# Sums of squares of the memory tokens moved from GpSimd to VectorE and to later attention steps, and one half projection moved between the first two steps

## The chip, the cores and the metric

One Trainium2 chip, one core of it. The metric is device time in microseconds (us) of one execution of the whole program, the median of a few runs. The engines that matter are TensorE (PE in the profile; its weight loads are PEld), VectorE (DVE), ScalarE (ACT), GpSimd (POOL) and the queue from which transfers are issued (SP). Each engine takes its own instructions in the order in which they stand in its queue, and an instruction that waits for another engine holds up all that stand behind it.

## The reference, cut to what matters

```python
h = rms_norm(x, norm_mix)                       # x: 512 tokens of 1024
q_a, k_a, v_a, u_b, gate_b, gate_c, g_a, g_b = split(h @ w_in)
o_a = stick_breaking_attention(q_a, k_a, v_a)   # 8 heads of 64, causal
y_b = gate_b * conv3(gate_c * u_b)
merged = sigmoid(g_a) * (o_a @ w_branch_a) + sigmoid(g_b) * (y_b @ w_branch_b)
x = x + merged @ w_mix_out
x = x + memory_cross_attention(rms_norm(x, norm_mem_q), rms_norm(mem, norm_mem_kv), ...)
x = x + swiglu(rms_norm(x, norm_ffn));  return rms_norm(x, norm_final)

# stick-breaking weights, z = q.k / 8, s < t:
# A[t,s] = exp(log_sigmoid(z_ts) + sum over s<j<t of log_sigmoid(-z_tj))

# rms_norm(mem): mem is 256 tokens of 1024, so for each token the mean of its
# 1024 squares is needed
```

Everything is float32. The change concerns two things in it: where and when the squares of `mem` are summed, and when the projections `h @ w_in` are made that lie between the steps of the attention.

## The kernel before, in words

A float32 operand of a matmul is split into a rounded part "hi" and the rest "lo" (two instructions, a cast on ScalarE and a subtraction on VectorE: L150 and L151 for weights, L169 and L170 for activations, L369 and L370 inside the attention), and a product is made of three matmuls, hi·hi, hi·lo and lo·hi (`mm3`, L155 to L157).

**The attention** runs over `steps` (L341): 4 pairs of heads, and for each pair the four key blocks `kt` = 3, 2, 1, 0, so 16 steps, numbered 0 to 15. Key block `kt` is met by queries from `kt`·128 on: 128, 256, 384 or 512 queries for each head. Up to 256 queries both heads of a pair share one PSUM bank `z`; above that each head has its own. For one step the work is this:

- `scores` (L373): matmuls into `z` (L382 or L389); then on ScalarE Abs, Exp and Ln (L396 to L398), on VectorE the softplus `e` (L399), on GpSimd the causal mask on `e` (`affine_select`, L355); ScalarE copies row 0 of `z` to a small carry (L406).
- `parts` (L408): VectorE adds the carry of the key block before (L420), then `e` is split into `l` hi (ScalarE, L369) and `l` lo (VectorE, L370).
- `weights` (L428): for each bank two matmuls with a triangle of -1, first with `l` hi, then with `l` lo (L433); VectorE forms the carry (L438) which a small DMA moves (L444); ScalarE takes Exp (L441), GpSimd masks (L355), VectorE splits the result `a` into `ah` and `al` (L449, L450).
- `values` (L454): the matmuls with v (L461).

In the main loop (L519) step `i` issues, in this order: a share of projections (`fill_some`, L524), `scores` of step i+1, `weights` of step i, `parts` of step i+1, `values` of step i-1. So the chain from the scores of a step to its `l` lo lies beside the projections that stand between them in TensorE's queue. The queue of TensorE is in the order written (`manual_schedule`, L518); those of the other engines are ordered by the Tile scheduler.

**The projections** are a list `fill` of 44 entries (L492 to L505): for each projection one entry that loads its weights and makes the first four of eight k-blocks (`open_project`, 12 matmuls, L270) and one that makes the other four (12 matmuls) and evicts on VectorE. The order is q and k of the next pair (`qk_part`, evicted by L294), then for the convolution gate C, u and gate B (`conv`: L315; L321, L322, L324, L328; L334, L335). `FILL` (L33) says how many entries stand in front of each step: (3, 2, 3, 3) for the first pair, (2, 2, 3, 4) for the other three. The 44 shares add up to the 44 entries, so a share is a number of entries. q and k of the second pair take entries 0 to 3, gate C entries 4 and 5. Before, step 0 has the whole of q and the first half of k; step 1 the second half of k and the first half of gate C.

**The memory squares** (`mem_square`, L480): at the steps in `MEM_AT` (L30: 1, 3, 5, 7) a quarter of `mem` (128x512: two blocks of 128x256) is loaded through SP (L477), squared on ScalarE in place (L484) and added to `accm` (128x256) on GpSimd, block by block (a copy, L487, and seven adds, L489). At step 12 (`MEAN_AT - 2`, L523) `squares_mean` splits `accm` (L180, L181) and the mean is made of it at step 14.

Of the kernel before, what the change touches and what calls it, by code (L numbers as in the profile page):

```python
# [8 lines left out]
F32 = mybir.dt.float32  # L9
F32R = mybir.dt.float32r  # L10
AF = mybir.ActivationFunctionType
ALU = mybir.AluOpType

P = 128
D = 1024
S = 512
KD = D // P
# [4 lines left out]
MEM = 256  # L22
MT = MEM // P
# [3 lines left out]
HS = S // 2  # L27
EPS = 1e-6
HOLD = 4
MEM_AT = (1, 3, 5, 7)  # L30
MEAN_AT = 14
EARLY = 2
FILL = ((3, 2, 3, 3), (2, 2, 3, 4))  # L33
WARM = 8
FIRST = 4

# [4 lines left out]
def hybrid_layer(ctx: ExitStack, tc: tile.TileContext, xT_d, memT_d, cols_d, wv_d, win_d,  # L41
                 wbr_d, wmix_d, wmq_d, wmk_d, wmv_d, wmo_d, wfi_d, wfo_d, out):
    nc = tc.nc
# [10 lines left out]
    lpool = stick.enter_context(tc.tile_pool(name="lpool", bufs=4))  # L54
# [8 lines left out]
    def unit(s, cols=512):  # L63
        return upool.tile([P, cols], F32R, tag="u", name=nm(s), padded_shape=[P, 512])
# [4 lines left out]
    def f(ap):  # L69
        return ap.bitcast(F32)  # L70
# [42 lines left out]
    def rstd_of(var, n, s, tables=(), eps=True, keep=None):  # L113


        def new(t):
            return tmp(t, n) if n > TT else spool.tile([P, n], F32, tag=t, name=nm(t))

        v, y, a = (new("rv") if keep is None else keep) if eps else var, new("ry"), new("ra")
        r = cpool.tile([P, n], F32, tag=s, name=nm(s))  # L120
        after(nc.scalar.activation(y, var, AF.Ln, bias=eps_t if eps else 0.0), tables)
        if eps:
            if n > TT:
                nc.vector.tensor_scalar(out=v, in0=var, scalar1=EPS, scalar2=None, op0=ALU.add)
            else:
                nc.scalar.activation(v, var, AF.Identity, bias=eps_t)
        exps.append(nc.scalar.activation(y, y, AF.Exp, scale=-0.5))
        nc.vector.tensor_tensor(out=a, in0=y, in1=y, op=ALU.mult)
        nc.vector.scalar_tensor_tensor(out=a, in0=a, scalar=-0.5, in1=v, op0=ALU.mult,
                                       op1=ALU.mult)  # L130
        nc.vector.scalar_tensor_tensor(out=r, in0=a, scalar=1.5, in1=y, op0=ALU.add, op1=ALU.mult)
        return r
# [44 lines left out]
    def squares_mean(acc, n):  # L177

        parts = unit("acch", n * P), unit("accl", n * P)
        nc.vector.tensor_copy(parts[0], acc)  # L180
        nc.vector.tensor_tensor(out=parts[1], in0=acc, in1=f(parts[0]), op=ALU.subtract)  # L181

        def by_token(s, tables=(), bank=otile):

            vp = bank("var")
            for t in range(n):
                for i in range(2):
                    nc.tensor.matmul(vp[:, 2 * t:2 * t + 2], parts[i][:, t * P:(t + 1) * P],
                                     mean_r[:, 0:2], start=i == 0, stop=i == 1)
            return rstd_of(vp[:, 0:2 * n].rearrange("p (t two) -> p t two", two=2)[:, :, 0], n, s,  # L190
                           tables)

        def along(s, tables=(), bank=otile, keep=None):

            vp = bank("varb")[:, :n * P]
            for i in range(2):
                nc.tensor.matmul(vp, mean_r, parts[i], start=i == 0, stop=i == 1)
            return rstd_of(vp, n * P, s, tables, keep=keep)

        return by_token, along  # L200
# [103 lines left out]
    def gate(m, j):  # L304
        ps = project((O_A, O_B)[j] + m * P)
        t = gates[m, j] = tmp("g")
        nc.vector.tensor_tensor(out=t, in0=ps, in1=r0b, op=ALU.mult)
# [65 lines left out]
    def scores(p, kt):  # L373
        c0, n = span(kt)
        q, k = qk[p]
        ks = slice(kt * P, (kt + 1) * P)
        terms = (0, 0), (0, 1), (1, 0)
        if 2 * n <= 512:
            zs[p, kt] = [ztile("z")[:, :2 * n]]
            z3 = by_head(zs[p, kt], kt)[0]  # L380
            for i, (a, b) in enumerate(terms):
                nc.tensor.matmul(z3, k[a][:, ks], late_q[p % 2][b][:, :, c0 - HS:],  # L382
                                 start=i == 0, stop=i == 2)
        else:
            zs[p, kt] = [ztile("z")[:, :n] for _ in range(2)]
            for i, (a, b) in enumerate(terms):
                for h in range(2):
                    hs = slice(h * HD, (h + 1) * HD)
                    nc.tensor.matmul(zs[p, kt][h], k[a][hs, ks], q[b][hs, c0:],  # L389
                                     start=i == 0, stop=i == 2)  # L390
        es[p, kt] = []
        with tc.high_priority(100):
            for h, z in enumerate(zs[p, kt]):
                w = z.shape[1]
                e = tmp("e")[:, :w]
                nc.scalar.activation(e, z, AF.Abs)  # L396
                nc.scalar.activation(e, e, AF.Exp, scale=-1.0)
                nc.scalar.activation(e, e, AF.Ln, bias=1.0)  # L398
                nc.vector.scalar_tensor_tensor(out=e, in0=z, scalar=0.0, in1=e, op0=ALU.max,  # L399
                                               op1=ALU.add)  # L400
                causal(by_head([e], kt)[0])
                es[p, kt].append(e)
                if kt > 0:
                    r = carries[kt % 2][0:1, h * w:(h + 1) * w]
                    first.setdefault((p, kt), []).append(r)
                    nc.scalar.copy(r, z[0:1, :])  # L406

    def parts(p, kt):  # L408


        c0, n = span(kt)
        sp[p, kt] = []
        with tc.high_priority(100):
            for h, e in enumerate(es.pop((p, kt))):
                w = e.shape[1]
                if kt < TT - 1:
                    c = carries[(kt + 1) % 2][P - 32:P, h * w // n * (n - P):]
                    c = c[:, :w // n * (n - P)].rearrange("p (h n) -> p h n", n=n - P)
                    e3 = e.rearrange("p (h n) -> p h n", n=n)[P - 32:P, :, P:]
                    nc.vector.tensor_tensor(out=e3, in0=e3, in1=c, op=ALU.add)  # L420
                sp[p, kt].append(lsplit(e, w, f"l{kt % 2}"))
# [49 lines left out]
                                        op=ALU.add)  # L471
            oT.append(split(t, "o"))

    accm = lpool.tile([P, MEM], F32, tag="accm", name="accm", bufs=1)

    def load_mem(k2, t):
        nc.sync.dma_start(t, memT_d[2 * k2 * P:(2 * k2 + 2) * P, :].rearrange("(j p) t -> p j t",  # L477
                                                                              p=P))

    def mem_square(k2):  # L480

        mk = f(unit("mk")).rearrange("p (j t) -> p j t", j=2)
        load_mem(k2, mk)
        nc.scalar.activation(mk, mk, AF.Square)  # L484
        for j in range(2):
            if k2 + j == 0:
                nc.gpsimd.tensor_copy(accm, mk[:, j, :])  # L487
            else:
                nc.gpsimd.tensor_tensor(out=accm, in0=accm, in1=mk[:, j, :], op=ALU.add)  # L489


    fill = []  # L492
# [13 lines left out]
    n_fill = len(fill)  # L506
    shares = FILL[0] + (TT - 1) * FILL[1]

    def fill_some(to):
        while fill and n_fill - len(fill) < to:  # L510
            g, *args = fill.pop(0)
            g(*args)
# [5 lines left out]
    with tc.manual_schedule(engines={mybir.EngineType.PE}):  # L518
        for i in range(len(steps) + 1):  # L519
            if i in MEM_AT:  # L520
                mem_square(MEM_AT.index(i))
            if i == MEAN_AT - 2:
                mean = squares_mean(accm, MT)  # L523
            fill_some(n_fill * sum(shares[:i + 1]) / sum(shares))  # L524
            if i == MEAN_AT:
                rm = mean[0]("rm", bank=mmtile)
            if i + 1 < len(steps):
                scores(*steps[i + 1])
            if i < len(steps):
                weights(*steps[i])  # L530
            else:
                gate(EARLY, 0)
            if i + 1 < len(steps):
                parts(*steps[i + 1])
            if i > 0:
                values(*steps[i - 1])
            if i == MEAN_AT:
                rmb = mean[1]("rmb", bank=mmtile)
# [143 lines left out]
    for h in range(MH):  # L682
# [12 lines left out]
        for t2 in range(2):  # L695
# [6 lines left out]
                                           in1=r1s[:, 2 * t2:2 * t2 + 2], op0=ALU.mult,  # L702
# [10 lines left out]
            for i in range(2):  # L713
                nc.vector.tensor_scalar(out=pr[:, i * MEM:(i + 1) * MEM],
                                        in0=pr[:, i * MEM:(i + 1) * MEM],
# [253 lines left out]
    with tc.manual_schedule(engines={mybir.EngineType.PE, mybir.EngineType.Activation,  # L969
# [5 lines left out]
        for n in range(2 * KD):  # L975
# [13 lines left out]
            elif n == KD + 1:  # L989

                nc.vector.scalar_tensor_tensor(out=sq[1, 0], in0=eps_sq[:, sl], scalar=D / P,
                                               in1=sq[1, 0], op0=ALU.mult, op1=ALU.add)
# [34 lines left out]
    for j in range(KD // 2):  # L1027
        y = yg[0, j]
        nc.gpsimd.tensor_tensor(out=y, in0=y, in1=rf0[:, None, :].broadcast_to([P, 2, hs]),
                                op=ALU.mult)  # L1030
# [63 lines left out]
```

## Time and profile before

| what | value |
|---|---|
| median of 3 runs | 861.97 us (861.52 to 862.36) |
| the profiled execution, its time | 862.82 us |
| its span (first to last instruction) | 861.1 us |
| PE busy | 851.6 us of the span, 4912 matmuls |
| DVE, ACT, POOL busy | 587.1, 431.3, 69.7 us |
| attention steps 0 to 15 | from 43 to 195 us of the span, roughly |

The profile gives each instruction's start from the beginning of the span, its duration, its line in the kernel, and the tiles it writes and reads (`out<-in`, buffer numbers left out). Behind a row of the timeline stands, in brackets, how long the engine was idle before it and what ended that. Matmuls are pipelined: a row of 0.39 us is followed by the next matmul 0.23 us later, so distances between starts are what counts on PE.

### The profile page before, as it was taken

The numbers are of one execution on the slowest core, as the hardware profiler recorded it, in microseconds if no ns is written. First come the engines' busy times: TensorE is split into PE (matmuls) and PEld (weight loads), VectorE is DVE, ScalarE is ACT, GpSimd is POOL, SyncE is SP. The second block draws the span as 40 slices with busy tenths as digits, with TensorE's granted clock in tenths as the row PEclk, the third lists the DMA queues.
The fourth block names the chain that finished last, engine by engine and source line by source line (L and its number), as shares of the span: only waits on it lengthen the run. The fifth ranks groups of instructions, "written<-read, shape, count | busy, mean of one in ns | idle before, by whom it ended". The sixth has DMA issues, their size and how long they took to land.

```text
span 861.1 us, 12693 instructions
## 1 busy us (share of the span) xinstructions
PE 851.6 (99%) x4912; PEld 749.1 (87%) x4912; DVE 587.1 (68%) x959; ACT 431.3 (50%) x750; POOL 69.7 (8%) x100
## 2 busy tenths in 40 slices
PE   9999999999999999999999999999999999999997
PEld 7877788888888898888888889999999999888897
DVE  8769898986455466555555879888887788533334
ACT  7566766565333344443444656555445556322335
POOL 1023131111000000000000100111111100000002
PEclk9999999999999999999999999999999999999999
DMA  8332331228333355433111427777677763333202
GB/s 294 129 104 86 99 117 55 74 83 269 113 110 110 98 161 190 150 99 96 52 51 48 134 51 199 187 185 176 177 190 188 192 148 127 118 98 99 73 1 98
DMA packets 42859, 108.34 MB, mean 126 GB/s; under 512 B 4656, under 2 KB 8752, under 8 KB 42800
## 3 DMA queue, kind: packets, MB, share of 16 engines
q1 hardware_dynamic: 36528, 95.72, 34.1%
q0 software_dynamic: 5984, 11.54, 8.4%
q8 instruction: 38, 0.62, 0.3%
q10 hardware_dynamic: 288, 0.29, 0.1%
q14 instruction: 21, 0.17, 0.1%
HBM read 104.36 MB, written 2.10 MB: 124 GB/s over the span
## 4 chain that ended last, share of the span: by engine, by line
PE 96%; DVE 2%; DMA 0%; issue 0%; POOL 0%; DVEq 0%; SPq 0%; ACT 0%; POOLq 0%
PE z L801 15%; PE y L801 7%; PE pr L155 7%; PE pr L156 7%; PE pr L157 7%; PE f L157 5%; PE f L155 5%; PE f L156 5%; PE v L801 4%; PE r L156 3%; PE r L157 3%; PE r L155 3%; PE v L261 3%; PE mq L157 2%; PE mq L156 2%; PE mq L155 2%
## 5 line engine op out<-in xcount | busy, mean ns | idle before, releaser
L150 ACT CAST wh<-wr 128x1024 fp32r<-128x1024 f32 x106 | 111.2, 1052 | 221.5 <-issue 98.6
L151 DVE TENSOR_TENSOR wl<-wr,wh 128x1024 fp32r<-128x1024 f32 x106 | 129.4, 1223 | 99.6 <-ACT wh L150 99.2
L155 PE MATMUL pr<-xgh,wh 128*128 128x512 f32 x288 | 112.5, 391 | 0.0
L156 PE MATMUL pr<-xgl,wh 128*128 128x512 f32 x288 | 112.3, 390 | 0.0
L157 PE MATMUL pr<-xgh,wl 128*128 128x512 f32 x288 | 112.2, 390 | 0.0
L156 PE MATMUL f<-actl,wh 128*128 128x512 f32 (+1 forms) x208 | 74.2, 357 | 0.0
L155 PE MATMUL f<-acth,wh 128*128 128x512 f32 (+1 forms) x208 | 74.2, 357 | 0.0
L157 PE MATMUL f<-acth,wl 128*128 128x512 f32 (+1 forms) x208 | 74.0, 357 | 0.0
L801 PE MATMUL z<-xdh,wf 128*128 128x256 f32 x352 | 70.3, 283 | 0.0
L758 POOL DMA_DIRECT2D ws<-in_w_ffn_in_dram x22 | 26.6, 1208 | 468.6 <-DVE c L616 267.8
L157 PEld LDWEIGHTS pr<-xgh,wl 128*128 128x128 f32 x288 | 54.1, 188 | 11.3
L155 PEld LDWEIGHTS pr<-xgh,wh 128*128 128x128 f32 x288 | 54.1, 188 | 11.0
L156 PEld LDWEIGHTS pr<-xgl,wh 128*128 128x128 f32 x288 | 54.1, 188 | 10.9
L801 PEld LDWEIGHTS z<-xdh,wf 128*128 128x128 f32 x352 | 58.0, 192 | 0.0
L821 ACT COPY sa<-z 128x256 f32<-128x256 f32 x44 | 16.4, 373 | 78.2 <-PE z L801 78.1
L801 PE MATMUL z<-xdl,wf 128*128 128x256 f32 x176 | 49.8, 283 | 0.0
L792 DVE TENSOR_TENSOR wf<-s,wf 128x512 fp32r<-128x512 f32 x44 | 30.3, 691 | 21.0 <-ACT wf L791 20.0
L155 PEld LDWEIGHTS f<-acth,wh 128*128 128x128 f32 x208 | 39.3, 189 | 5.7
L156 PEld LDWEIGHTS f<-actl,wh 128*128 128x128 f32 x208 | 39.3, 189 | 5.6
L157 PEld LDWEIGHTS f<-acth,wl 128*128 128x128 f32 x208 | 39.3, 189 | 5.6
L801 PE MATMUL v<-xoh,wf 128*128 128x256 f32 x176 | 35.5, 283 | 0.0
L801 PE MATMUL y<-xch,wf 128*128 128x256 f32 x176 | 35.5, 283 | 0.0
(280 smaller groups left out, 2144.4 us busy)
## 6 DMA issues: line engine op xcount, KB each, us to landing
wr<-in_w_in_dram SPq DMA_DIRECT2D x36, 512.0 KB, 3.4
ws<-in_w_ffn_in_dram SPq DMA_DIRECT2D x22, 512.0 KB, 3.8
wg<-in_w_ffn_in_dram SPq DMA_DIRECT2D x22, 512.0 KB, 4.4
ws<-in_w_ffn_in_dram POOLq DMA_DIRECT2D x22, 512.0 KB, 5.9
wr<-in_w_ffn_out_dram SPq DMA_DIRECT2D x22, 512.0 KB, 3.3
a<-in_w_ffn_in_dram SPq DMA_DIRECT2D x22, 256.0 KB, 4.7
wr<-in_w_branch_dram SPq DMA_DIRECT2D x8, 512.0 KB, 3.5
wr<-in_w_mem_k_dram SPq DMA_DIRECT2D x8, 512.0 KB, 3.4
```

What stands on the lines that cost most here:

```text
L150: after(nc.scalar.copy(h2, raw), lead[-1:])
L151: lows.append(nc.vector.tensor_tensor(out=l2, in0=raw, in1=f(h2), op=ALU.subtract))
L155: nc.tensor.matmul(ps, a[0], b[0], start=start, stop=False, **kw)
L156: nc.tensor.matmul(ps, a[0], b[1], start=False, stop=False, **kw)
L157: nc.tensor.matmul(ps, a[1], b[0], start=False, stop=stop, **kw)
L261: nc.tensor.matmul(vps[t], xg[k][a][:, sl], wv[k][b], start=k == 0 and (a, b) == (0, 0), stop=k == KD - 1 and a == 1)
L758: nc.gpsimd.dma_start(s13, a[:, 0:4:3, :], accum_op=ALU.add)
L792: nc.vector.tensor_tensor(out=lo, in0=raw, in1=f(hi), op=ALU.subtract)
L801: nc.tensor.matmul(ps[:, :HS], a, b, start=i < 3 and k == 0 and j == 0, stop=k == KP - 1 and j == 2, skip_group_check=True)
L821: nc.scalar.copy((s[:, :HS], None, None, s[:, HS:], t[:, :HS])[i], z)
```

## The change: what it does

```diff
-MEM_AT = (1, 3, 5, 7)
+MEM_AT = (5, 7, 9, 11)
-FILL = ((3, 2, 3, 3), (2, 2, 3, 4))
+FILL = ((2, 3, 3, 3), (2, 2, 3, 4))
...
-    accm = lpool.tile([P, MEM], F32, tag="accm", name="accm", bufs=1)
+    accm = lpool.tile([P, 2, MEM], F32, tag="accm", name="accm", bufs=1)
...
         mk = f(unit("mk")).rearrange("p (j t) -> p j t", j=2)
         load_mem(k2, mk)
-        nc.scalar.activation(mk, mk, AF.Square)
-        for j in range(2):
-            if k2 + j == 0:
-                nc.gpsimd.tensor_copy(accm, mk[:, j, :])
-            else:
-                nc.gpsimd.tensor_tensor(out=accm, in0=accm, in1=mk[:, j, :], op=ALU.add)
+        nc.scalar.activation(accm if k2 == 0 else mk, mk, AF.Square)
+        if k2 > 0:
+            nc.vector.tensor_tensor(out=accm, in0=accm, in1=mk, op=ALU.add)
+        if k2 == KD // 2 - 1:
+            nc.vector.tensor_tensor(out=accm[:, 0, :], in0=accm[:, 0, :], in1=accm[:, 1, :],
+                                    op=ALU.add)
...
-                mean = squares_mean(accm, MT)
+                mean = squares_mean(accm[:, 0, :], MT)
```

The four quarters of the memory are now loaded and squared at steps 5, 7, 9 and 11. ScalarE writes the first squares straight into `accm`, which is twice as wide; the other three are added to it by VectorE, 128x512 at a time, and after the fourth VectorE adds the two halves. GpSimd has no part in it any more. In the first pair, step 0 has two entries of projections in front of it instead of three, and step 1 three instead of two: the first half of k of the second pair (12 matmuls) moves from in front of the scores of step 1 to behind the weights of step 0.

The order of the instructions on each engine, as built, shows what else moves. TensorE: only those 12 matmuls. ScalarE: around the same place the cast of q (L169) and the next weight cast (L150) come some places later, and the four squares move. VectorE: around steps 0 and 1 `l` lo of step 1 stands ahead of the eviction of k and of a weight subtraction instead of behind them; the three new adds stand, first, in step 7 between the two `l` lo (there the product L335 moves behind the second), second, in step 9 ahead of L420, third, in step 11 ahead of a weight subtraction, with the add of the halves behind that. SP: the four loads of `mem` move with their steps; at step 0 the small copies of q of the second pair (L300) stand behind the carry's copy instead of around it. Step 3's order is unchanged on every engine but for the squares that are gone from it.

## The prediction, made before the changed kernel ran

> **What bounds the kernel now.** I read the page first: the engines' busy time and the chain that ended last.
>
> ```profile
> PE 851.6 (99%) x4912; PEld 749.1 (87%) x4912; DVE 587.1 (68%) x959; ACT 431.3 (50%) x750; POOL 69.7 (8%) x100
> PE 96%; DVE 2%; DMA 0%; issue 0%; POOL 0%; DVEq 0%; SPq 0%; ACT 0%; POOLq 0%
> ```
>
> TensorE is busy for 851.6 of 861.1 us and holds 96% of the chain. The change takes no matmul away and adds none, so it can only alter the time in which TensorE waits. The view of waits, for PE alone, has one line beside that of the program's start (us in total, times, longest):
>
> ```profile
> PE z L433 <- DVE l L370: 2.1, 2, 1.5
> ```
>
> That is what the change can win: two waits of the triangle matmuls for `l` lo. The timeline of PE shows where, and what an undisturbed passage looks like (the rows from 170.40 are the same step of the fourth pair):
>
> ```profile
> 56.45 0.49 PE L433 MATMUL z<-l,negtri 128*128 128x512 f32 x1
> 57.49 0.50 PE L433 MATMUL z<-l,negtri 128*128 128x512 f32 x1 [0.54 <-DVE l L370]
> 57.83 0.22 PE L461 MATMUL o<-ah,v 128*128 128x128 f32 x1
> ...
> 170.40 0.73 PE L433 MATMUL z<-l,negtri 128*128 128x512 f32 x2
> 170.97 0.22 PE L461 MATMUL o<-ah,v 128*128 128x128 f32 x1
> ...
> 77.26 1.02 PE L433 MATMUL z<-l,negtri 128*128 128x512 f32 x3
> 79.81 0.50 PE L433 MATMUL z<-l,negtri 128*128 128x512 f32 x1 [1.53 <-DVE l L370]
> 80.16 0.33 PE L461 MATMUL o<-ah,v 128*128 128x384 f32 x1
> ...
> 155.16 1.09 PE L433 MATMUL z<-l,negtri 128*128 128x512 f32 x4
> 156.10 0.33 PE L461 MATMUL o<-ah,v 128*128 128x384 f32 x1
> ```
>
> Step 1: from the first L433 to the first L461 are 57.83 - 56.45 = 1.38 us, undisturbed 170.97 - 170.40 = 0.57: **0.81 us lost**. Step 3: 80.16 - 77.26 = 2.90, undisturbed 156.10 - 155.16 = 0.94: **1.96 us lost**. Together 2.77 us, 0.32% of the time, and no more is to be had in the attention.
>
> **Step 0: what the moved half projection covered.** In these rows stands step 0 as it is, on PE, ACT, POOL and DVE:
>
> ```profile
> 46.12 0.40 PE L155 MATMUL pr<-xgh,wh 128*128 128x512 f32 x1
> 48.86 0.62 PE L382 MATMUL z<-lq,qkh 128*128 128x512 f32 x2
> 49.55 0.76 PE L433 MATMUL z<-l,negtri 128*128 128x256 f32 x2
> 50.14 0.40 PE L155 MATMUL pr<-xgh,wh 128*128 128x512 f32 x1
> ...
> 45.22 0.39 ACT L396 ACTIVATE e<-z 128x256 f32<-128x256 f32 x1 [3.41 <-PE z L382]
> 46.41 1.04 ACT L150 CAST wh<-wr 128x1024 fp32r<-128x1024 f32 x1
> 49.00 0.41 ACT L369 CAST l<-e 128x256 fp32r<-128x256 f32 x1 [0.78 <-POOL e L355]
> ...
> 47.48 1.49 POOL L355 TENSOR_SCALAR_AFFINE_SELECT e<-e 128x256 f32<-128x256 f32 x1 [42.81 <-DVE e L399]
> ...
> 46.92 0.42 DVE L399 SCALAR_TENSOR_TENSOR e<-z,e 128x256 f32<-128x256 f32 x1
> 47.48 1.23 DVE L151 TENSOR_TENSOR wl<-wr,wh 128x1024 fp32r<-128x1024 f32 x1
> 49.44 0.43 DVE L370 TENSOR_TENSOR l<-e,l 128x256 fp32r<-128x256 f32 x1 [0.74 <-ACT l L369]
> ```
>
> The first half of k runs from 46.12 to 48.86, 2.74 us; then come the scores of step 1 and at 49.55 the triangle of step 0. `l` is just ready then. The chain that makes it is Abs at 45.22, softplus at 46.92, the mask from 47.48 to 48.97, hi at 49.00, lo from 49.44 to 49.87. Nothing in this chain depends on the half projection, and up to lo its instructions stand in the same order on POOL and VectorE; on ScalarE the Abs of step 1 comes in ahead of the hi cast (it can start when the cast at 46.41 ends, at 47.45, for some 0.6 us, an estimate from 0.39 for half the columns) and is through before the mask ends. So lo is ready at 49.87 as before. But TensorE, 12 matmuls lighter, comes to the triangle at 49.55 - 2.74 = 46.81 and stands still until 49.5. At 50.14 it starts the first half of k instead of the second. **Cost: +2.74 us**, as one gap of some 2.6 us.
>
> The least cost: if every instruction of the chain followed the one before at once, with Exp and Ln as long as Abs and the mask at 0.53 us (the same select at 52.76, below), lo would be done at 45.22 + 3 x 0.39 + 0.42 + 0.53 + 0.41 + 0.43 = 48.18, 1.69 before 49.87; then the move costs 1.05 us. The queues don't allow that, since VectorE takes the weight subtraction (47.48 to 48.71) ahead of lo.
>
> The mask took 1.49 us beside that subtraction, and 0.53 in this row, where VectorE did something else:
>
> ```profile
> 52.76 0.53 POOL L355 TENSOR_SCALAR_AFFINE_SELECT e<-e 128x256 f32<-128x256 f32 x1 [1.00 <-DVE e L399]
> ```
>
> Both start at 47.48. Should the mask go first in a run, it ends at 48.01; the subtraction, held until then, ends at 48.01 + 1.23 = 49.24, and lo at 49.24 + 0.43 = 49.67: 0.20 us less, +0.65 instead of the +0.85 below. The Trainium skill (SBUF — State Buffer, "Who interferes with whom") says that a VectorE instruction with two SBUF inputs and a GpSimd instruction that reads SBUF exclude each other, and that whichever starts first keeps the port to its end; by that rule either order is possible here. The trace agrees so far as the mask ended 0.26 us after the subtraction did.
>
> **Step 1: the moved half as new cover.** From 50.14 to the triangle at 56.45 TensorE now has 6.31 us of work; it will have 6.31 + 2.74 = 9.05 and reach it at 59.19. `l` lo of step 1 needs the scores of step 1, 2.74 us earlier now, and the carry of step 0, at the same time as before. VectorE takes it ahead of the eviction of k, so it isn't later than now, when TensorE gets it at 57.49: 1.7 us before it will ask. **-0.81 us.** After it the eviction of k and all that follows in VectorE's queue come some 2 us later, as TensorE does.
>
> **Step 3: GpSimd's adds go.** The end of step 3 on VectorE and GpSimd, and below it the same instructions in the third pair, where no memory square stands:
>
> ```profile
> 66.64 0.69 DVE L321 TENSOR_TENSOR cu<-pr,r0b 128x512 f32<-128x512 f32 x1 [1.18 <-PE pr L157]
> 76.81 0.68 DVE L370 TENSOR_TENSOR l<-e,l 128x512 fp32r<-128x512 f32 x1
> 77.40 1.23 DVE L335 TENSOR_TENSOR gb<-gb,cv 128x512 f32<-128x512 f32 x1
> 78.56 1.21 DVE L370 TENSOR_TENSOR l<-e,l 128x512 fp32r<-128x512 f32 x1
> ...
> 76.92 2.29 POOL L489 TENSOR_TENSOR accm<-accm,mk 128x256 f32<-128x256 f32 x2 [1.17 <-ACT mk L484]
> ...
> 150.96 0.69 DVE L370 TENSOR_TENSOR l<-e,l 128x512 fp32r<-128x512 f32 x1
> 151.56 0.69 DVE L335 TENSOR_TENSOR gb<-gb,cv 128x512 f32<-128x512 f32 x1
> ```
>
> Beside GpSimd's two adds (76.92 to 79.21) L335 and the second lo took 1.23 and 1.21 us; alone 0.69 each, starting 0.60 apart. Without the adds: L335 at 77.40, lo at 78.00 to 78.69 instead of 79.77: **-1.08 us**. It doesn't get better than that, because VectorE works through from 66.64, when TensorE hands over u, to here without a break that counts, and TensorE, later by then, hands u over later by as much. So 1.96 - 1.08 = 0.88 us of the wait stay.
>
> **The new adds on VectorE** aren't in the trace. The nearest rows are L335, 0.69 us for 128x512 with two SBUF inputs, and L370 at 49.44, 0.43 for 128x256: 3 x 0.69 + 0.43 = 2.5 us, against nothing if all lie in slack. I take nothing, by these rows:
>
> ```profile
> 116.00 1.22 DVE L370 TENSOR_TENSOR l<-e,l 128x512 fp32r<-128x512 f32 x1
> 117.20 1.09 PE L433 MATMUL z<-l,negtri 128*128 128x512 f32 x4
> ...
> 138.57 1.03 DVE L370 TENSOR_TENSOR l<-e,l 128x384 fp32r<-128x384 f32 x2 [0.29 <-ACT l L369]
> 142.62 0.97 PE L433 MATMUL z<-l,negtri 128*128 128x384 f32 x4
> ...
> 159.70 0.43 DVE L370 TENSOR_TENSOR l<-e,l 128x256 fp32r<-128x256 f32 x1
> 162.97 0.40 PE L433 MATMUL z<-l,negtri 128*128 128x256 f32 x2
> ```
>
> In step 7 lo ends at 117.22, just in time, but it is stretched there by GpSimd's adds as in step 3; the new add takes L335's place ahead of it and GpSimd's go, so lo ends earlier. In step 9 lo ends at 139.60, 3.0 us before TensorE begins the triangle; the add of step 11 and that of the halves, 1.1 us, lie ahead of a lo that ends 2.8 us before its use. If that cover were gone, what waits behind is the triangle and so TensorE, at up to 2.5 us. The loads of `mem` in SP's queue (a weight load stands behind each) and the squares on ScalarE move along with the adds, as many as before; they lie beside the projections of steps 5 to 11, where TensorE doesn't wait once. Uncovered, a square would cost the 0.6 us of any 128x512 pass on ScalarE. I take both at nothing.
>
> **The sum:** 2.74 - 0.81 - 1.08 = **+0.85 us**. Against its own execution that is 862.82 + 0.85 = 863.67; that execution lies 0.85 above the median of the runs, 861.97, and the forecast goes by the median: **862.8 us**, +0.1%. A measurement of this kernel can tell about 0.2% from no change, 1.72 us: faster is below 860.25, slower above 863.69.
>
> **The rivals.**
>
> *Step 3 gives nothing back*: another thing ends last there, say VectorE's queue comes later by more than TensorE. For it speaks that VectorE is full for 13 us before; against it, that both stretched rows lie exactly beside the adds. 862.8 + 1.08 = 863.9, slower; chance 0.14.
>
> *The clock falls in the new gap.* At the program's start matmuls are slower:
>
> ```profile
> 1.61 3.78 PE L220 MATMUL warm<-neg 128*128 128x512 f32 x8 [1.61 <-DVE neg L87]
> 7.00 1.17 PE L261 MATMUL v<-wvl,xgh 128*128 128x512 f32 x4
> ```
>
> 12 matmuls took 7.00 - 1.61 = 5.39 us, against 2.74 for 12 at 46.12. If the gap of 2.6 us sets TensorE back to that, 2.65 us are paid once more right after it: 865.5, slower. The idle 1.53 at 79.81 did not do it (the L461 behind it took 0.33, as at 156.10), so it decides between 1.5 and 2.6 us of idleness. The Trainium skill (TensorE: Matmul & The Clock Gate, "What's actually happening") puts the point at one idle window of about 3.4 us; by that rule the gap is too short and nothing is paid. Chance 0.07.
>
> *The wait at step 0 is shorter*: mask and subtraction change places, or the chain draws together. Between 862.6 and, with the least cost of 1.05, 861.97 + 1.05 - 1.89 = 861.1; with step 3 quite free besides, 860.25. Chance 0.11, of which 0.03 fall below that.
>
> *The new adds find no cover*, or wait for squares that come late: up to 862.8 + 2.5 = 865.3; chance 0.10, 0.07 of it slower.
>
> **How the numbers follow.** The forecast has 0.58 (0.03 of it above 863.69, since runs of one kernel spread over 0.84 us), step 3 lost 0.14 (0.10 slower), the clock 0.07, the shorter wait 0.11, the uncovered adds 0.10. Slower: 0.03 + 0.10 + 0.07 + 0.07 = 0.27; faster 0.03; the same 0.70. The range goes from the shorter wait, less some noise, 861.5, to step 3 lost with noise, 864.4; the clock, most of the uncovered adds and the tails, under 0.2, stay out.
>
> **What would show it.** In the changed profile: PE waiting some 2.6 us at the triangle of step 0, near 49.5, for hi or lo; none at step 1; under 1 us at step 3; L335 at 0.69 in all four pairs. The forecast is wrong if the scores of step 1 are followed by projections ahead of that triangle, if matmuls after 50.14 are over 0.23 us apart, or if a wait stands in steps 7 to 12.

## The result and the profile after

The changed kernel takes **864.59 us** (median of 10 runs, 863.53 to 865.2) against 862.25 us before (10 runs, 861.52 to 862.87): ratio 1.0026, 95% interval 1.0018 to 1.0035. It is slower by 2.3 us where +0.85 was forecast, and the time lies 0.2 us above the top of the forecast's range. The forecast stood on 861.97 us, the median of three runs of before; ten runs give 862.25, so 0.3 us of the difference to the forecast's 862.8 come from there, and 1.5 us have to be explained.

The profiled execution is the fastest of the ten, 863.53 us, 0.71 above the profiled one of before. In it what was forecast for steps 0, 1 and 3 can be found. The waits of TensorE (us in total, times, longest):

```profile
PE z L433 <- ACT l L369: 2.5, 1, 2.5
PE warm L220 <- DVE neg L87: 1.6, 1, 1.6
PE z L433 <- DVE l L370: 0.5, 1, 0.5
```

The timeline of TensorE at steps 0, 1 and 3:

```profile
46.01 0.62 PE L382 MATMUL z<-lq,qkh 128*128 128x512 f32 x2
46.47 0.40 PE L382 MATMUL z<-lq,qkl 128*128 128x512 f32 x1
49.34 0.84 PE L433 MATMUL z<-l,negtri 128*128 128x256 f32 x2 [2.48 <-ACT l L369]
50.03 0.40 PE L155 MATMUL pr<-xgh,wh 128*128 128x512 f32 x1
...
59.02 0.73 PE L433 MATMUL z<-l,negtri 128*128 128x512 f32 x2
59.59 0.22 PE L461 MATMUL o<-ah,v 128*128 128x128 f32 x1
...
79.03 1.02 PE L433 MATMUL z<-l,negtri 128*128 128x512 f32 x3
80.52 0.51 PE L433 MATMUL z<-l,negtri 128*128 128x512 f32 x1 [0.47 <-DVE l L370]
80.87 0.33 PE L461 MATMUL o<-ah,v 128*128 128x384 f32 x1
```

Step 0: from the scores of step 1 to the next projection 50.03 - 46.01 = 4.02 us, before 50.14 - 48.86 = 1.28, so +2.74. Step 1: 59.59 - 59.02 = 0.57, the undisturbed length, so -0.81. Step 3: 80.87 - 79.03 = 1.84, before 2.90, so -1.06. And on VectorE: the `l` lo of step 1, step 3, and the new adds of steps 7, 9 and 11:

```profile
55.17 0.69 DVE L370 TENSOR_TENSOR l<-e,l 128x512 fp32r<-128x512 f32 x1 [0.74 <-ACT l L369]
...
79.18 0.69 DVE L335 TENSOR_TENSOR gb<-gb,cv 128x512 f32<-128x512 f32 x1
79.78 0.68 DVE L370 TENSOR_TENSOR l<-e,l 128x512 fp32r<-128x512 f32 x1
...
115.33 0.69 DVE L486 TENSOR_TENSOR accm<-accm,mk 128x512 f32<-128x512 f32 x1
115.93 0.69 DVE L370 TENSOR_TENSOR l<-e,l 128x512 fp32r<-128x512 f32 x1
...
138.04 0.77 DVE L486 TENSOR_TENSOR accm<-accm,mk 128x512 f32<-128x512 f32 x1
...
156.05 0.69 DVE L486 TENSOR_TENSOR accm<-accm,mk 128x512 f32<-128x512 f32 x1
156.65 1.22 DVE L151 TENSOR_TENSOR wl<-wr,wh 128x1024 fp32r<-128x1024 f32 x1
157.78 0.42 DVE L488 TENSOR_TENSOR accm<-accm 128x256 f32<-128x256 f32 x1
```

At step 3 L335 and lo are back at 0.69 and 0.68, and no wait of TensorE stands where the new adds are.

So this profile doesn't show why the other nine executions take longer. What tells of it is the granted TensorE clock, the share of full speed that the chip let TensorE run at, of which the mean over the execution is recorded with each:

| time, us | 863.53 | 863.85 | 863.9 | 864.27 | 864.55 | 864.63 | 864.7 | 864.72 | 864.86 | 865.2 |
|---|---|---|---|---|---|---|---|---|---|---|
| clock | 0.999 | 0.999 | 0.999 | 0.997 | 0.997 | 0.998 | 0.998 | 0.997 | 0.996 | 0.996 |

Three executions have 0.999 and lie near 863.8; the other seven are slower and have less. That led back to the second rival of the prediction, that the clock falls in the new gap.

### The profile page after: what moved, and what is told of

Read it like the earlier page. It is cut to its first block, busy times and chain, and to the rows that moved or that the text cites. A ratio compares the mean times of both kernels' runs of the same rounds, so it can differ in the third digit from the quotient of the medians.

```text
span 861.8 us, 12692 instructions
## 1 busy us (share of the span) xinstructions
PE 851.5 (99%) x4912; PEld 749.2 (87%) x4912; DVE 586.5 (68%) x963; ACT 430.8 (50%) x750; POOL 61.9 (7%) x92
## 4 chain that ended last, share of the span: by engine, by line
PE 97%; DVE 2%; POOL 0%; issue 0%; DVEq 0%; ACT 0%; POOLq 0%
PE z L801 15%; PE y L801 7%; PE pr L155 7%; PE pr L156 7%; PE pr L157 7%; PE f L157 5%; PE f L155 5%; PE f L156 5%; PE v L801 4%; PE r L155 3%; PE r L157 3%; PE r L156 3%; PE v L261 3%; PE mq L155 2%; PE mq L157 2%; PE mq L156 2%
## 5 line engine op out<-in xcount | busy, mean ns | idle before, releaser
L150 ACT CAST wh<-wr 128x1024 fp32r<-128x1024 f32 x106 | 111.0, 1050 | 221.3 <-issue 98.6
```

What stands on the lines that cost most here:

```text
L150: after(nc.scalar.copy(h2, raw), lead[-1:])
```

## The experiments

Two theories stood against each other. **A:** the clock falls in the gap of 2.5 us at step 0, in most executions but not in the one first profiled. **B:** some other wait, differing between executions, makes the seven slower. The changed kernel again, the filled gap, the squares alone and the shares alone were measured together (before: 862.55 us there), the other four together (before: 862.69).

**The changed kernel again, for another profile.** No edit.

> The changed kernel once more. The profiled execution was 863.53 us, 0.71 above the profiled one of before, as the forecast's terms had it (+0.85), but it was the fastest of ten; the median was 864.59, and the executions above it had granted clocks of 0.996 to 0.998 against its 0.999. Theory A, the clock falls in the new 2.5 us gap in most executions: the times fall in two groups, near 863.6 at clock 0.999 and 0.9 to 1.7 us above at 0.996 to 0.998, and a profile taken in the second group shows the clock at half somewhere between 47 and 54 us and matmuls over 0.4 us apart there. Theory B, the extra comes from waits elsewhere that vary between executions: such a profile shows a wait of TensorE of about 1 us in another step, with the clock up.

Measured: 864.92 us (863.75 to 865.24, 7 runs), 1.0027 (1.0016 to 1.0038). This time the profiled execution is one of the slower, 865.21 us at clock 0.996. Busy times by stretch (columns: stretch, its length, then PE, PEld, DVE, ACT and POOL busy with counts, the granted clock, the DMA engines' share, GB/s), in stretches of 3.41 us counted back and forth from the point at which the clock changes:

```profile
44.22:47.64 3.42, 2.71 (x13) 1.92 (x11) 1.24 (x3) 2.41 (x5) 0.21 (x1) 1.00 0.45 147
47.64:51.05 3.41, 1.57 (x7) 1.20 (x8) 2.20 (x4) 2.59 (x7) 1.27 (x1) 1.00 0.37 120
51.05:54.46 3.41, 3.41 (x10) 2.67 (x9) 1.58 (x5) 0.73 (x2) 0.81 (x2) 0.50 0.29 82
54.46:57.88 3.42, 3.42 (x17) 2.81 (x16) 1.61 (x3) 1.36 (x2) 0.00 (x0) 1.00 0.15 36
```

and the matmuls at the start of the third and at its end:

```profile
50.09 0.40 PE L155 MATMUL pr<-xgh,wh 128*128 128x512 f32 x1
...
51.83 0.63 PE L155 MATMUL pr<-xgh,wh 128*128 128x512 f32 x1
52.25 0.63 PE L156 MATMUL pr<-xgl,wh 128*128 128x512 f32 x1
...
54.88 0.39 PE L157 MATMUL pr<-xgh,wl 128*128 128x512 f32 x1
```

The wait at step 0 is the same 2.48 us as in the first profile. But 1.6 us after TensorE has taken up work again (at 49.41), at 51.05, the clock goes to 0.50, for one stretch of 3.41 us; the matmuls start 0.43 apart instead of 0.23. The 14 distances from 50.09 to 54.88 take 4.79 us; at 0.228 each they would take 3.19: **1.6 us**. The span is 863.5 us, 1.7 above the first profile's. The only other difference in the view of waits is one of 0.2 us at the start (L261). That is theory A, in this execution. One stretch at half clock takes 3.41 x 0.5 / 862 = 0.002 off the mean clock. The profiles without a fall in mid-run have 0.998 to 1.000, since in each the clock is halved near the end as well, behind the last matmul, where it costs TensorE nothing. So, as far as these profiles show, 0.997 or less tells of a fall in mid-run: eight of the 17 executions of the changed kernel have 0.996 or 0.997, and of the 94 executions of kernels without the gap whose clock is on record (50 of before, 11 each of the filled gap, the squares alone, the squares later and both waits, below) none has less than 0.998. Five more have 0.998 and are as slow; for these only the time speaks. Together 13 of 17 lie above 864.2 us.

**The gap filled.** Nine matmuls of constants between the scores of step 1 and the triangle of step 0, which nothing reads:

```diff
+            if i == 0:
+                idle = otile("idle")
+                for _ in range(9):
+                    nc.tensor.matmul(idle, neg1, neg1[:, None, :].broadcast_to([P, S // P, P]),
+                                     start=True, stop=True)
             if i < len(steps):
                 weights(*steps[i])
```

> The changed kernel with nine matmuls of constants (128x512, into a spare bank, about 2.1 us, read by nothing) put into the gap ahead of the triangle of step 0; all else is as in the changed kernel and lo isn't later. Theory A: the clock stays up in all executions, 0.999, and the median falls by 1.0 to 1.5 us to 863.1 to 863.5, which is the forecast's sum. Theory B: the median stays at 864.5, since the gap's length and all other waits are the same.

Measured: 863.07 us (862.68 to 863.65, 11 runs), 1.0007 (0.9998 to 1.0015). The triangle of step 0 still waits for `l`:

```profile
45.24 0.62 PE L382 MATMUL z<-lq,qkh 128*128 128x512 f32 x2
45.70 0.39 PE L382 MATMUL z<-lq,qkl 128*128 128x512 f32 x1
45.93 2.23 PE L532 MATMUL idle<-neg 128*128 128x512 f32 x9
48.57 0.84 PE L433 MATMUL z<-l,negtri 128*128 128x256 f32 x2 [0.41 <-ACT l L369]
49.25 0.40 PE L155 MATMUL pr<-xgh,wh 128*128 128x512 f32 x1
```

From the scores to the next projection it takes 49.25 - 45.24 = 4.01 us, as long as with the gap. No useful matmul runs earlier; only the idleness is gone, and 1.85 us with it (864.92 - 863.07). All 11 executions lie within 1 us, with clocks of 0.998 and 0.999. Theory B falls. What is left against before is +0.5 us by the medians. The profiles tell it more closely when they are compared from a matmul behind the start, here the first L382, before, in the first profile of the changed kernel and with the gap filled:

```profile
43.44 0.28 PE L382 MATMUL z<-lq,qkh 128*128 128x256 f32 x1
```

```profile
43.33 0.28 PE L382 MATMUL z<-lq,qkh 128*128 128x256 f32 x1
```

```profile
42.56 0.28 PE L382 MATMUL z<-lq,qkh 128*128 128x256 f32 x1
```

From there to the end of the span (861.1, 861.8 and 861.0 us) are 817.7, 818.5 and 818.4 us: +0.8 in both, the forecast's sum. In the profile with the fall the same distance is 863.5 - 43.39 = 820.1, 1.6 more.

**Three matmuls in the gap instead of nine**, so that 1.8 us of it stay idle (`range(3)` in the edit above).

> The changed kernel with three matmuls of constants in the gap ahead of the triangle of step 0, so that 1.8 us of idleness are left instead of 2.5. In the execution where the clock fell it was at half for one stretch of 3.41 us, from 51.05 to 54.46, and such stretches counted back from there lay over the idle 46.9 to 49.4 so that one of them, 47.64 to 51.05, was idle for 1.8 us, half of it; where it did not fall, the longest idle share of a stretch was 1.44 us. Theory A1, the clock falls when about half of a stretch (1.5 to 1.8 us) was idle: with 1.8 us in all this is met only if the whole gap falls into one stretch, so in under half of the executions, and the median is near the filled gap's 863.1 with single ones 1.5 us above. Theory A2, any gap of this order drops the clock in most executions: median 864.3 to 864.9, as with 2.5 us.

Measured: 863.88 us (863.05 to 865.41, 11 runs), 1.0016 (1.0007 to 1.0025). The wait that is left:

```profile
PE z L433 <- ACT l L369: 1.8, 1, 1.8
```

Eight executions lie from 863.05 to 863.89 with clocks of 0.998 or more, three above 864.2 (864.24, 864.51 and 865.41, with 0.997, 0.998 and 0.996), against 13 of 17 with the whole gap. So a gap of 1.8 us drops the clock seldom, one of 2.5 us mostly (A1; three of eleven is a small number, and no profile shows one of the three). The profiled one is of the eight. The median is 0.8 us above the one expected. In the two profiles that difference lies ahead of the first L382, which starts at 43.34 here and at 42.56 with the gap filled; from there to the end both take 818.5 us within 0.1. Whether the others of the eight start later too, and why, is open.

**The gap lengthened**: a further half projection moved away.

```diff
-FILL = ((2, 3, 3, 3), (2, 2, 3, 4))
+FILL = ((1, 4, 3, 3), (2, 2, 3, 4))
```

> The changed kernel with one more half projection taken from in front of step 0 (shares 1, 4, 3, 3): TensorE comes to the triangle of step 0 up to 2.7 us earlier still, so the gap is 3.5 to 5 us. Terms of the sum: up to +2.7 over the changed kernel with the clock up (863.6 on its own), 866.3, a little less where lo comes earlier because the eviction of q no longer stands ahead of the softplus. Theory A: the clock falls in every execution, for one or two stretches of 3.41 us, 1.6 us each: 867 to 869, and no execution has a clock above 0.998. Without a fall: 866 and 0.999.

Measured: 867.86 us (867.14 to 868.75, 4 runs), 1.0065 (1.0051 to 1.0079). The gap is shorter than expected, 3.0 us, with another 0.7 just ahead of it, in which the scores wait for a small copy of q:

```profile
PE z L433 <- ACT l L369: 3.0, 1, 3.0
PE z L382 <- DMA lq<-qkl: 0.7, 1, 0.7
```

Busy times by stretch of the profiled execution (868.35 us, clock 0.995):

```profile
44.77:48.19 3.42, 0.74 (x4) 0.30 (x3) 0.42 (x1) 2.99 (x8) 0.41 (x1) 1.00 0.35 137
48.19:51.60 3.41, 2.87 (x7) 2.19 (x8) 1.73 (x5) 1.26 (x4) 0.94 (x2) 0.50 0.01 2
51.60:55.01 3.41, 3.41 (x9) 2.64 (x9) 0.42 (x1) 0.39 (x1) 0.00 (x0) 0.50 0.00 0
55.01:58.40 3.39, 3.39 (x17) 2.79 (x16) 3.29 (x5) 1.80 (x3) 0.00 (x0) 1.00 0.13 30
```

Two stretches at half clock, the second although TensorE was busy in it throughout and for 2.87 of 3.41 us in the one before. The clock came back one whole busy stretch later. The other three executions have a clock of 0.994 each, so the clock fell in all four.

**The squares alone**: the shares as before, all else of the change.

```diff
-FILL = ((2, 3, 3, 3), (2, 2, 3, 4))
+FILL = ((3, 2, 3, 3), (2, 2, 3, 4))
```

> Only the memory squares changed (VectorE, steps 5 to 11), the shares of projections as before. By the forecast's term for step 3, -1.1 us against before: 861.2, the wait at step 3 down from 1.5 to under 0.6 us idle, L335 at 0.69 in all four pairs; the wait of step 1 stays at 0.5 idle. Theories A and B agree here, since there is no new gap. If the term of step 3 is wrong, the time stays at 862.2.

Measured: 861.37 us (860.42 to 862.1, 11 runs), 0.9985 (0.9976 to 0.9994): faster by 1.2 us, as forecast for step 3. Its profiled execution has a clock of 0.998 with no fall in the attention: the clock is at half only from 857.0 us on, and from 856 on TensorE has no matmul left. So 0.998 by itself doesn't tell; in the table above the times and the clocks speak together. TensorE's waits for lo, at steps 1 and 3:

```profile
PE z L433 <- DVE l L370: 1.0, 2, 0.6
```

**The shares alone**: the kernel before with `FILL = ((2, 3, 3, 3), (2, 2, 3, 4))`.

> Only the shares changed, the memory squares as before. By the forecast's terms 2.74 - 0.81 = +1.9 us: 864.2. Theory A: that holds for executions at clock 0.999, the median is 1.0 to 1.5 us more, 865.2 to 865.7. Theory B: 864.2 if the varying waits lie where the new adds are, in steps 5 to 12.

Measured: 865.39 us (864.89 to 865.76, 5 runs), 1.0035 (1.0022 to 1.0049): slower by 2.8 us, 0.9 more than the two terms give. The profiled one, 865.03 us at clock 0.999, has the gap (2.5) and the wait of step 3 (1.6) and no fall; from the first L382 to the end it takes 863.3 - 43.71 = 819.6 us, 1.9 more than before, as the two terms say. The five times are too close together to part them into two groups, but the clocks part them: the three slowest (865.39 to 865.76) have 0.997, the other two 0.999. So three of five fell, by the clock; none of the three is profiled.

**The squares later, but still on GpSimd**: the kernel before with one line changed.

```diff
-MEM_AT = (1, 3, 5, 7)
+MEM_AT = (5, 7, 9, 11)
```

> The kernel before with the squares moved to steps 5, 7, 9 and 11 and nothing else: GpSimd still adds them. Tells whether the gain at step 3 comes from the time or from the engine. If only the absence of adds at step 3 counts: L335 and lo at 0.69 there, stretched to 1.2 in steps 7 and 11, where lo has 0.7 and 4 us of slack: the time is that of the squares on VectorE, 861.4, -1.1 against before. If GpSimd's adds cost elsewhere too: between 861.4 and 862.5.

Measured: 861.64 us (861.05 to 862.31, 11 runs), 0.9990 (0.9981 to 0.9999), -1.05 us. At step 3 the gain is one of time, not of the engine: L335 and lo take 0.68 and 0.69 us there and the wait is 0.47, as with the adds on VectorE, so it comes from there being no adds beside step 3. By the medians the difference to the adds on VectorE (-1.2) is within both intervals. But the profile has one wait more than theirs:

```profile
PE z L433 <- DVE l L370: 1.3, 3, 0.6
```

The third, 0.58 us, stands at 170.05 in step 13, where lo starts 0.66 us later than in the squares alone, counted from the first L382 (169.31 - 43.30 against 169.05 - 43.70). Whether GpSimd's adds cause it, and in how many executions, is open.

**Both waits, without the gap.** The squares on VectorE, and the cover for step 1 taken from step 2 instead of step 0:

```diff
-FILL = ((2, 3, 3, 3), (2, 2, 3, 4))
+FILL = ((3, 3, 2, 3), (2, 2, 3, 4))
```

> The squares on VectorE, and shares (3, 3, 2, 3): step 0 keeps its three, and the half projection for step 1's wait is taken from step 2, where lo lay 2.6 to 2.7 us ahead of its use. Expected: the wait of step 1 gone (-0.8 against 861.4), step 2 just without one, step 3's wait at 0.5 idle as it is, no gap at step 0 and the clock at 0.999: 860.6. The rival: lo of step 2 comes late by some tenths, or step 3's wait grows since u reaches VectorE no earlier: 861.4 or above.

Measured: **860.93 us** (860.64 to 861.45, 11 runs), 0.9982 (0.9974 to 0.9991), 1.8 us faster than before, the fastest of all. TensorE's waits in the attention are down to this line:

```profile
PE z L433 <- DVE l L370: 0.5, 1, 0.5
```

The wait of step 1 is gone and step 2 has got none, as expected: its last lo is ready at 65.72 us, 0.5 ahead of its triangle at 66.24, where before it was 2.0 (65.46 against 67.43).

## Why the prediction was wrong

- *The cost at step 0, +2.74 us as one gap:* right to the hundredth (4.02 - 1.28), and lo came at the same time as before.
- *Step 1, -0.81 us:* right (0.57 left of 1.38); lo was ready 3.2 us ahead of the triangle (55.17 + 0.69 = 55.86, against 59.02) instead of the 1.7 given as a bound.
- *Step 3, -1.08 us:* right (-1.06), in the changed kernel and alone (-1.2 with the squares only).
- *The new adds at nothing:* right; they took 0.69, 0.77, 0.69 and 0.42 us and made no wait.
- *The sum, +0.85:* this is what an execution takes more whose clock stays up: +0.8 from the first L382 on, in the first profile and with the gap filled. Its terms hold.
- *The failed step: the gap was priced at its length alone.* The prediction set out from the change having as many matmuls as before, so that it "can only alter the time in which TensorE waits", and put a change of the clock at nothing in the sum. It did alter the speed of the matmuls behind the gap: at half clock for one stretch of 3.41 us, which costs 1.6 us, and that is the usual case, 13 of 17 executions. The rival "the clock falls in the new gap" had named the place and the cause, but was given 0.07. The median belongs to the case with the fall: with +0.85 and 1.6 the estimate would have been 862.25 + 2.45 = 864.7, where 864.59 was measured. The rival's price was off as well: 2.65 us had been read from the program's start.
- Against that rival stood the idle 1.53 us of step 3 that had no effect. In that profile the stretches, counted from the first record of the clock, meet at 78.86 us and cut this wait (78.28 to 79.81) into 0.58 and 0.95; it could say little of a longer idleness within one stretch.
- The Trainium skill (TensorE: Matmul & The Clock Gate, "What's actually happening") has the clock fall after at least one idle window of about 3.4 us. The length of the window agrees with these runs (3.41 us at half clock), but it need not be idle from end to end. In the profile with the fall the stretch ahead of it, 47.64 to 51.05, holds idleness only up to 49.41, 1.77 us, about half.

The first profile shows why an execution can escape. The trace's record of the clock begins at the point at which the first matmuls get faster. In both profiles with a fall the fall comes a whole number of stretches behind it: from 6.68 to 51.05 us are 13 x 3.413, and with the longer gap from 7.23 to 48.19 are 12 x 3.413. In the first profile the record begins at 6.95, and stretches laid from there cut the same gap otherwise:

```profile
44.49:47.90 3.41, 2.38 (x12) 1.64 (x10) 1.56 (x3) 2.73 (x6) 0.53 (x1) 1.00 0.32 125
47.90:51.32 3.42, 1.90 (x8) 1.49 (x9) 2.21 (x5) 2.42 (x6) 1.07 (x2) 1.00 0.41 156
51.32:54.73 3.41, 3.41 (x17) 2.83 (x16) 1.66 (x4) 0.79 (x2) 0.70 (x2) 1.00 0.23 51
```

Here the gap ends at 49.34, and 1.44 us of it lie in the stretch from 47.90, 1.03 in the one ahead. Neither is enough. The profile of the shares alone says the same, and its wait of 1.55 us at step 3 lies whole in one stretch (third row), with the clock up behind it too:

```profile
45.33:48.75 3.42, 1.92 (x9) 1.22 (x7) 2.03 (x3) 2.90 (x6) 1.00 (x1) 1.00 0.24 98
48.75:52.16 3.41, 2.36 (x10) 1.86 (x11) 2.19 (x6) 2.25 (x5) 0.89 (x2) 1.00 0.46 161
79.47:82.88 3.41, 1.86 (x9) 1.18 (x9) 3.41 (x4) 1.91 (x5) 2.69 (x3) 1.00 0.00 0
```

That the point lies between 1.55 and 1.8 us of 3.41 is read from these profiles and the times with three matmuls in the gap; where exactly, and whether idleness is counted just so, stays open.

## What to carry to other kernels

Moving cover from a step that just has enough to one that lacks some makes a gap nearly as long as the piece moved (2.48 us for 2.74): take it from a step with slack instead (here step 2, whose lo was ready 2.0 us ahead of its triangle). A gap on TensorE can cost more than its length: here 1.77 us of idleness in one stretch of 3.41 us put the matmuls behind it at half clock for the next such stretch, and 1.55 us did not. Count that in for gaps of this order, and fill such a gap with matmuls that nothing reads if it can't be avoided. When a change makes such a gap, one profile is no sample: compare the granted clocks of several executions before trusting its time.

## What the runs showed of the hardware that was not expected

- **The fall comes late and by the stretch.** In the profile with the fall TensorE was idle from about 46.9 to 49.4 us, yet the clock fell at 51.05, in the midst of dense matmuls, and came back exactly 3.41 us later.
- **The start differs from execution to execution.** The matmuls at the start run some 0.45 us apart until the trace's record of the clock begins, from where they run 0.23 apart, and that moment differs: 7.18 us before, 5.19 with the gap filled. The mean clock says nothing of it, since the granted clock reads 1.00 from 0 to 7 us in both. Before, and with the gap filled:

```profile
5.18 2.02 PE L261 MATMUL v<-wvh,xgh 128*128 128x512 f32 x4
7.00 1.17 PE L261 MATMUL v<-wvl,xgh 128*128 128x512 f32 x4
```

```profile
5.18 1.15 PE L261 MATMUL v<-wvh,xgh 128*128 128x512 f32 x4
6.18 1.08 PE L261 MATMUL v<-wvl,xgh 128*128 128x512 f32 x4
```

The same four matmuls take 1.82 us from start to start in one and 1.00 in the other: 0.8 us of difference before anything else has happened. In nine profiles (all but the lengthened gap's, where the order of the matmuls is another) the first L382 starts between 42.56 and 43.71 us; the ten runs of before lie within 1.35 us. That the scatter of each kernel comes from there is likely, but not shown by one or two profiles of a kernel. By this, profiles should be compared from a point behind the start.
